# Eleven instead of seven pairs of the down projection with seven multiplications, their weight differences and token sums made in an earlier stage

## The chip, the core and the metric

The kernel runs on one core of a Trainium2 chip. The metric is the time of one execution on the device in microseconds (us); lower is better. Of the core's engines, TensorE (PE) multiplies 128x128 blocks, VectorE (DVE) and ScalarE (ACT) work on elements, GpSimd (POOL) and SyncE (SP) issue transfers (DMAs); "PEld" in the profile is PE's loading of the stationary operand.

## What is computed

One decoder block on 256 tokens and 16 meta tokens of width 2048: a recurrent branch and an attention branch, merged by gates and projected by `w_o`, and then a feed-forward part of width 5632. The change touches the last line of the reference, and uses what the line before it makes:

```python
h = h + merged @ w_o
gate, up = jnp.split(_rms(h, n2) @ w_gu, 2, axis=-1)
return h + (jax.nn.silu(gate) * up) @ w_dn        # w_dn: 5632 x 2048, float32
```

## The kernel before

**Split operands.** All matmuls run on float32r operands that are split in two: a high part (ACT copies float32 to float32r, `wh`) and a low part (DVE subtracts the high part from the float32 value, `wl`). A product of two such operands is three matmuls: high x high, low x high, high x low. Weights come from memory in raw tiles of 128x1024 float32 (512 KB; tag `raw`, four buffers), loaded by SP, and are split into `wh` and `wl` (four buffers each). `wload` (line 314) does this for a plain job, `split` for others.

**Jobs.** `run` takes a list of pairs (load, mul). It calls the load of a job and then the mul of the job before it. PE works in the order of the program. The orders of DVE, ACT, SP and POOL are made by the scheduler of the tile framework, so that loads and splits of later jobs stand well ahead of PE. Side work is written as generators: `spawn` starts one with a delay, each `yield` gives the time until its next step, and `slot`, called at each product, advances a clock made of the matmuls' own lengths and runs a step that has come due. This clock only decides where in the program the step is written.

**Gate and up** (lines 1385 to 1402). For each of eleven blocks `j` of 512 columns, `cm_jobs` multiplies the normed tokens `hts` with 512 columns of gate and then of up: 16 jobs of 8 pairs of matmuls (128x512 and 128x256), one raw tile a job. `post_gate` and `post_up` take the sums out of PSUM, multiply by the norm and by silu of the gate and split the product into `ach` and `acl`, the operand of the down projection: 44 blocks of 128 rows, 256 tokens.

**Down projection** (lines 1410 to 1572). Its 44 row blocks are taken in 22 pairs; the 2048 result columns in two halves `cg` of 1024. A pair and a half is a product of 2x2 blocks: two halves of 128 tokens and two row blocks, times two row blocks (`b11 b12`, `b21 b22`) and two groups of 512 columns. A plain pair (`slow_jobs`) makes eight products, 24 matmuls of 128x512, in two jobs with one raw tile each. A fast pair (`fast_jobs`) makes seven, 21 matmuls, from sums and differences of the blocks, in four jobs: `mul0` one product, `mul1`, `mul2` and `mul3` two each. Four of the products go to four PSUM banks of their own (`ps`, tile names `dnp`), the others to the four banks of the plain sums (`cs`, tile names `dn`); at the end of a half `sums_of_products` adds the four into the result `hh` (a copy by ACT and eight additions by DVE), and `post` adds the plain sums and stores.

Before the change pairs 0 to 6 are fast. Their weights lie in two raw tiles (1 MB a pair and half), and DVE makes four differences of 512 columns into `tt` (line 1515) between the splits. The sums and differences of tokens are made by `sums_of_pairs` (lines 1417 to 1446) on DVE from the split operand, in four batches beside the first jobs of the down projection; they are split into `sst`, which takes the memory of `hts`. `ORDER` puts eight plain pairs first and then fast and plain pairs in turn in the first half, and two plain pairs for each fast one in the second.

Of the kernel before, what the change touches and what calls it, by code (L numbers as in the profile page):

```python
# [18 lines left out]
P = 128  # L19
D = 2048  # L20
NMETA = 16
# [20 lines left out]
for _n, _k in (("n1", 16), ("mu", 24), ("mu_w", 1), ("mu_a", 1), ("mu_g", 2), ("w0", 8), ("a0", 8), ("k_k", 8),  # L42
# [19 lines left out]

LANES = 108
# [4 lines left out]
FAST = [0, 1, 2, 3, 4, 5, 6]  # L68
BATCHES = (2, 2, 2, 1)
SLOW = list(range(7, 22))  # L70
ORDER = [SLOW[:8] + [i for pair in zip(FAST, SLOW[8:]) for i in pair],
         [i for n, f in enumerate(FAST) for i in (SLOW[2 * n], f, SLOW[2 * n + 1])] + SLOW[14:]]
# [44 lines left out]
def hybrid_block(ctx, tc, A, out, dbg=None):  # L117
# [195 lines left out]

    def wload(parts, n, between=None, lay=None):
# [6 lines left out]
        if lay is not None:  # L321
# [14 lines left out]
            nc.vector.tensor_tensor(tl, rr, th.bitcast(F32), op=ALU.subtract)  # L336
# [967 lines left out]
    hts = hp.tile([P, KT, 2, L], F32R, tag="hts", name="hts")  # L1304
# [32 lines left out]
    for j in range(4):  # L1337
# [3 lines left out]
        def post(t, ps, j=j, js=js):  # L1341
            nc.vector.tensor_tensor(hh[:, t, js], ps, hh[:, t, js], op=ALU.add)
            jk = hp.tile([P, 512], F32, tag="jk", name=f"jk{j}{t}", bufs=2)
# [3 lines left out]
            for k in range(4 * j, 4 * j + 4):  # L1347
                pt = aux_ps(f"hT{k}")[:, :T]
                for t in range(2):
                    nc.tensor.transpose(pt[:, t * P:(t + 1) * P], hh[:, t, k * P:(k + 1) * P], ident)  # L1350
                tmp = hp.tile([P, T], F32, tag="htmp", name=f"htmp{k}", bufs=3)
                nc.vector.tensor_scalar(tmp, pt, vc("n2", k), None, op0=ALU.mult)
                split(hts[:, k, 0, NMETA:], hts[:, k, 1, NMETA:], tmp)
# [6 lines left out]
    obs = [hp.tile([P, P], F32, tag="ob", name=f"ob{t}", bufs=2) for t in range(2)]  # L1360
# [19 lines left out]
    acp = ap_pool.__enter__()  # L1380
    NF = DFF // P
    ach = acp.tile([P, NF, T], F32R, tag="ach", name="ach")
    acl = acp.tile([P, NF, T], F32R, tag="acl", name="acl")
    wgu = A["w_gate_up"][0]
    for j in range(DFF // 512):
# [8 lines left out]
        def post_up(pss, gs=gs, j=j):  # L1394
            for m, (g, ps) in enumerate(zip(gs, pss)):
# [5 lines left out]
        run(cm_jobs(wgu[:, j * 512:(j + 1) * 512], KT, hts, NMETA, T, post_gate, name=f"gt{j}"))  # L1401
        run(cm_jobs(wgu[:, DFF + j * 512:DFF + (j + 1) * 512], KT, hts, NMETA, T, post_up, alloc=aux_ps, name=f"up{j}"))
# [7 lines left out]
    wdn = A["w_down"][0]  # L1410
# [3 lines left out]
    sst = hp.tile([P, KT, 2, L], F32R, tag="hts", name="sst").rearrange("p k a t -> p (k a t)")  # L1414
    sst = sst[:, :len(fast) * 6 * P].rearrange("p (i s a c) -> p i s a c", i=len(fast), s=3, a=2)

    def sums_of_pairs():

        at = 0
        for n in BATCHES:  # L1420
            fs, ps_ = slice(at, at + n), slice(fast[at], fast[at] + n)
            at += n
            h = lambda k, t: acp_h[:, ps_, k, t, :].bitcast(F32)
            l = lambda k, t: acp_l[:, ps_, k, t, :].bitcast(F32)
            f = [sst[:, fs, i, 1, :] for i in range(3)] + [acp_l[:, ps_, 0, 1, :]]
            hi = [sst[:, fs, i, 0, :] for i in range(3)] + [acp_h[:, ps_, 0, 1, :]]
            f32 = [hp.tile([P, T], F32, tag="ga", name=f"s{at}{i}", bufs=8)[:, :n * P].rearrange("p (i c) -> p i c", c=P)
                   for i in range(4)]

            def tt(i, x_, y_, op):  # L1430
                nc.vector.tensor_tensor(f32[i], x_, y_, op=op)
            tt(0, h(0, 1), h(1, 1), ALU.add)
            tt(0, f32[0], l(0, 1), ALU.add)
            tt(0, f32[0], l(1, 1), ALU.add)
            tt(1, f32[0], h(0, 0), ALU.subtract)
            tt(1, f32[1], l(0, 0), ALU.subtract)
            tt(2, h(0, 0), h(0, 1), ALU.subtract)
            tt(2, f32[2], l(0, 0), ALU.add)
            tt(2, f32[2], l(0, 1), ALU.subtract)
            tt(3, h(1, 0), f32[1], ALU.subtract)  # L1440
            tt(3, f32[3], l(1, 0), ALU.add)
            yield PAIRS
            for i in range(4):
                nc.scalar.activation(hi[i], f32[i], AF.Copy)
                nc.vector.tensor_tensor(f[i], f32[i], hi[i].bitcast(F32), op=ALU.subtract)
            yield PAIRS
# [41 lines left out]
    def fast_jobs(i, cg, cs, ps, end):  # L1488
        box = {}

        def b(k, x_):
            return wdn[i * 256 + k * P:i * 256 + (k + 1) * P, cg * 1024 + x_ * 512:cg * 1024 + (x_ + 1) * 512]

        def load0():
            ra, rb = (wp.tile([P, 1024], F32, tag="raw", name="raw", bufs=RAWB) for _ in range(2))
            nc.sync.dma_start(ra, wdn[i * 256:i * 256 + P, cg * 1024:(cg + 1) * 1024])
            for x_ in range(2):
                nc.sync.dma_start(rb[:, (1 - x_) * 512:(2 - x_) * 512], b(1, x_))
            box["r"] = rows(ra), rows(rb)
            w = split_tiles()  # L1500
            split(*(t[:, 0:2] for t in w), box["r"][0][:, 0:2])
            return w

        def load1():
            w = split_tiles()
            split(*w, box["r"][1])
            return w

        def load2():
            (b11, b12), (b22, b21) = ([r[:, 0:2], r[:, 2:4]] for r in box["r"])  # L1510
            w, v = split_tiles(), split_tiles()
            ts = [rows(hp.tile([P, 1024], F32, tag="tt", name="tt", bufs=2)) for _ in range(2)]
            t1, t2, t3, t4 = (t[:, 2 * n:2 * n + 2] for t in ts for n in range(2))
# [122 lines left out]
```

## Time and profile before

| | |
|---|---|
| time, median of 3 runs | 1520.99 us (1520.26 to 1521.58) |
| profiled execution, span on the core | 1517.7 us (the page gives no other time for it) |
| granted PE clock | 1.00 throughout |
| gate and up | 788 to 1278 us, PE busy 490.0 of 490.0 |
| down projection | 1278 to 1514 us, PE busy 235.1 of 236.0 |
| bytes moved | 283.32 MB, mean 187 GB/s |
| landing of a 512 KB weight load | 4.3 us (gate and up), 5.3 us (down), medians |

The span runs from the first to the last instruction on the core; the time of a run holds a little more. A line of the groups reads: line of the kernel, engine, operation, result<-operands, shape, count, then busy time in us and the mean of one in ns, then the idle time of the engine just ahead of such instructions and who ended it. A line of the waits reads: engine, what waits, its line <- for whom, then us in all, times, and the longest.

### The profile page before, as it was taken

How to read it: one execution, taken by the hardware profiler on the slowest of the kernel's cores; microseconds unless marked ns; L12 is line 12 of the kernel's file. 1: busy time of each engine (PE TensorE's matmuls, PEld its weight loads, DVE VectorE, ACT ScalarE, POOL GpSimd, SP SyncE). 2: the span in 40 equal slices, each digit the busy share in tenths (PEclk: the TensorE clock that was granted, in tenths of full speed). 3: DMA queues.
4: the chain of work that ended last, by engine and by line, in shares of the span. 5: the costliest groups of instructions: out<-in, count | busy, mean ns of one | idle time of the engine just before them, and what ended most of it. 6: DMA issues, size and time to landing. Idle time of an engine off the chain costs nothing.

```text
span 1517.7 us, 26174 instructions
## 1 busy us (share of the span) xinstructions
PE 1509.9 (99%) x10071; PEld 1339.5 (88%) x10071; DVE 1112.0 (73%) x2009; ACT 808.3 (53%) x1230; POOL 99.3 (7%) x182
## 2 busy tenths in 40 slices
PE   9999999999999999999999999999999999999998
PEld 9999999999989888998888888888888888887887
DVE  7888699689789857875665666566566658879776
ACT  7664565475465545644554555454455545554543
POOL 2112202202202000000000000000000000000000
PEclk9999999999999999999999999999999999999999
DMA  8557456646645757777566666666666666566664
GB/s 271 166 166 212 119 156 185 170 122 173 188 127 149 223 152 214 234 231 240 181 179 192 189 187 193 191 186 192 190 187 191 193 186 182 178 211 201 213 206 138
DMA packets 210365, 283.32 MB, mean 187 GB/s; under 512 B 24320, under 2 KB 129296, under 8 KB 210240
## 3 DMA queue, kind: packets, MB, share of 16 engines
q1 hardware_dynamic: 205344, 277.25, 61.9%
q10 hardware_dynamic: 4896, 4.40, 0.9%
q8 instruction: 79, 1.29, 0.3%
q14 instruction: 46, 0.38, 0.1%
HBM read 274.36 MB, written 7.24 MB: 186 GB/s over the span
## 4 chain that ended last, share of the span: by engine, by line
PE 95%; DVE 3%; DMA 1%; issue 1%; ACT 0%; SPq 0%; DVEq 0%; ACTq 0%
PE up L441 11%; PE gt L441 11%; PE zg L441 8%; PE gt L443 5%; PE up L443 5%; PE dn L1461 4%; PE dn L1460 4%; PE dn L1462 4%; PE zg L443 4%; PE f L441 2%; PE br L365 2%; PE br L366 2%; PE br L367 2%; PE f L365 2%; PE wo L1329 2%; PE wo L1331 2%
## 5 line engine op out<-in xcount | busy, mean ns | idle before, releaser
L336 DVE TENSOR_TENSOR wl<-raw,wh 128x1024 fp32r<-128x1024 f32 x460 | 561.9, 1226 | 281.3 <-ACT wh L335 280.6
L335 ACT ACTIVATE wh<-raw 128x1024 fp32r<-128x1024 f32 x460 | 486.5, 1059 | 470.2 <-PE up L441 118.9
L441 PE MATMUL gt<-hts,wh 128*128 128x512 f32 x704 | 242.9, 393 | 0.0
L441 PE MATMUL up<-hts,wh 128*128 128x512 f32 x704 | 242.7, 392 | 0.0
L443 PE MATMUL gt<-hts,wl 128*128 128x256 f32 x660 | 184.8, 280 | 0.0
L443 PE MATMUL up<-hts,wl 128*128 128x256 f32 x660 | 184.6, 280 | 0.0
L441 PE MATMUL zg<-xhl,wh 128*128 128x512 f32 x512 | 181.2, 399 | 0.0
L441 PEld LDWEIGHTS up<-hts,wh 128*128 128x128 f32 x704 | 130.0, 188 | 25.2
L441 PEld LDWEIGHTS gt<-hts,wh 128*128 128x128 f32 x704 | 129.9, 188 | 25.1
L443 PE MATMUL zg<-xhl,wl 128*128 128x256 f32 x480 | 134.3, 280 | 0.0
L443 PEld LDWEIGHTS up<-hts,wl 128*128 128x128 f32 x660 | 125.3, 190 | 1.8
L443 PEld LDWEIGHTS gt<-hts,wl 128*128 128x128 f32 x660 | 125.3, 190 | 1.8
L441 PEld LDWEIGHTS zg<-xhl,wh 128*128 128x128 f32 x512 | 94.3, 188 | 18.7 <-issue 0.7
L1460 PE MATMUL dn<-wh,ach 128*128 128x512 f32 x282 | 110.7, 393 | 0.0
L1461 PE MATMUL dn<-wh,acl 128*128 128x512 f32 x282 | 110.6, 392 | 0.0
L1462 PE MATMUL dn<-wl,ach 128*128 128x512 f32 x282 | 110.5, 393 | 0.0
L443 PEld LDWEIGHTS zg<-xhl,wl 128*128 128x128 f32 x480 | 90.9, 189 | 1.2
L365 PE MATMUL f<-xhl,wh 128*128 128x272 f32 x256 | 75.9, 296 | 0.0
L367 PE MATMUL f<-xhl,wl 128*128 128x272 f32 x256 | 73.6, 288 | 0.0
L366 PE MATMUL f<-xhl,wh 128*128 128x272 f32 x256 | 73.6, 288 | 0.0
L1462 PEld LDWEIGHTS dn<-wl,ach 128*128 128x128 f32 x282 | 52.9, 187 | 12.3 <-DVE wl L336 0.3
L1461 PEld LDWEIGHTS dn<-wh,acl 128*128 128x128 f32 x282 | 52.9, 188 | 12.0
(493 smaller groups left out, 3056.7 us busy)
## 6 DMA issues: line engine op xcount, KB each, us to landing
raw<-in_w_gate_up_dram SPq DMA_DIRECT2D x176, 512.0 KB, 4.3
raw<-in_w_in_dram SPq DMA_DIRECT2D x160, 512.0 KB, 3.9
raw<-in_w_down_dram SPq DMA_DIRECT2D x74, 512.0 KB, 5.0
raw<-in_w_o_dram SPq DMA_DIRECT2D x32, 512.0 KB, 4.3
raw<-in_w_branch_a_dram SPq DMA_DIRECT2D x16, 512.0 KB, 4.6
raw<-in_w_branch_b_dram SPq DMA_DIRECT2D x16, 512.0 KB, 5.0
raw<-in_w_down_dram SPq DMA_DIRECT2D x28, 256.0 KB, 4.6
zgd<-zg ACTq DMA_DIRECT2D x30, 128.0 KB, 3.8
```

The lines of the kernel that those rows point to most:

```text
L335: nc.scalar.activation(th, rr, AF.Copy)
L336: nc.vector.tensor_tensor(tl, rr, th.bitcast(F32), op=ALU.subtract)
L365: nc.tensor.matmul(ps, wh, ah, start=first, stop=False)
L366: nc.tensor.matmul(ps, wh, al, start=False, stop=False)
L367: nc.tensor.matmul(ps, wl, ah, start=False, stop=last)
L441: nc.tensor.matmul(ps.rearrange("p (a t) -> p a t", a=2), wh, act, start=first, stop=last)
L443: nc.tensor.matmul(ps[:, :T], wl, act[:, 0, :], start=False, stop=False)
L1329: nc.tensor.matmul(o, ah[:, kt, ts_], hi, start=first, stop=False)
L1331: nc.tensor.matmul(o, ah[:, kt, ts_], lo_, start=False, stop=last)
L1460: nc.tensor.matmul(o, a[0], hi, start=first, stop=False)
L1461: nc.tensor.matmul(o, a[1], hi, start=False, stop=False)
L1462: nc.tensor.matmul(o, a[0], lo_, start=False, stop=last)
```

## The change

- Fast pairs are 0 to 10, plain pairs 11 to 21 (`FAST`, `SLOW`). In each half a lead of plain pairs comes first (`LEAD`: two, then one). Then, after each half of a fast pair, the number of plain jobs that keeps the two kinds in step; two plain jobs come last.
- `sums_of_weights`, a generator that starts in the first block of up, makes the differences of weights for all 22 combinations of fast pair and half. POOL loads the four blocks (1 MB, in two DMAs with rows of 2 KB) into `r`; DVE makes three subtractions (1024, 512 and 512 columns) into `v`; POOL stores `v` (1 MB) to the memory of the chip (`ts`). `r` and `v` have one buffer each. Each subtraction is put behind the last weight split written by then (`tc.issue_after(behind[0].ins)`). The steps are written 11000, 2600, 2600 and 1600 ns of the program's clock apart.
- `sums_of_tokens`, called in `post_up` for each fast pair, makes the four sums and differences of tokens (128 columns each) on DVE from the float32 product, and POOL stores them (`ss`, 256 KB).
- In the down projection a fast pair has four raw tiles: `b11` (256 KB), `b22` and `b21` (512 KB), and two loads of differences from `ts` (512 KB each). There is no subtraction of weights there any more. `split_of_sums` loads the token sums by POOL into `sl` (two buffers, up to two pairs each) and splits them into `sst`.
- Memory pools: `hts` moves into a pool of its own, with the high and the low part in two separate stretches of 4112 elements; the first parts of the stage, `r`, `v` and later `sst` and `sl` use pools one after the other. The last job of up is finished ahead of the down projection's pool in the program.

```diff
-FAST = [0, 1, 2, 3, 4, 5, 6]
-BATCHES = (2, 2, 2, 1)
-SLOW = list(range(7, 22))
+FAST = list(range(11))
+BATCHES = (2, 2, 2, 2, 2, 1)
+SLOW = list(range(11, 22))
+LEAD = (2, 1)
+LANDED = 11000
+DIFFER = 2600
+STORED = 1600
...
-    hts = hp.tile([P, KT, 2, L], F32R, tag="hts", name="hts")
+    hts = ht.tile([P, HTS], F32R, tag="hts", name="hts")[:, :2 * HPART].rearrange("p (a e) -> p a e", a=2)
+    hts = hts[:, :, NMETA:].rearrange("p a (k t) -> p k a t", t=T)
...
+    def sums_of_weights():
+        for cg in range(2):
+            for i in FAST:
+                r = pre.tile([P, 2, 1024], F32, tag="r", name="r", bufs=1)
+                for x_ in range(2):
+                    nc.gpsimd.dma_start(r[:, :, x_ * 512:(x_ + 1) * 512],
+                                        kblock(wdn[i * 256:(i + 1) * 256, cg * 1024 + x_ * 512:cg * 1024 + (x_ + 1) * 512]))
+                yield LANDED
+                v = pre.tile([P, 2, 2, 512], F32, tag="v", name="v", bufs=1)
+                b21, b22 = r[:, 1, :512], r[:, 1, 512:]
+                with tc.issue_after(behind[0].ins):
+                    nc.vector.tensor_tensor(v[:, 0], r[:, :, 512:], r[:, 0].rearrange("p (x c) -> p x c", x=2),
+                                            op=ALU.subtract)
+                yield DIFFER
+                with tc.issue_after(behind[0].ins):
+                    nc.vector.tensor_tensor(v[:, 1, 0], b22, v[:, 0, 0], op=ALU.subtract)
+                yield DIFFER
+                with tc.issue_after(behind[0].ins):
+                    nc.vector.tensor_tensor(v[:, 1, 1], b21, v[:, 1, 0], op=ALU.subtract)
+                d = tsd[i, cg] = dp.tile([4, P, 512], F32, tag=f"ts{i}{cg}", name=f"ts{i}{cg}")
+                nc.gpsimd.dma_start(d.rearrange("n p c -> p n c"), v.rearrange("p n x c -> p (n x) c"))
+                yield STORED
...
+        def load1():
+            r = fresh()
             for x_ in range(2):
-                nc.sync.dma_start(rb[:, (1 - x_) * 512:(2 - x_) * 512], b(1, x_))
+                nc.sync.dma_start(r[:, (1 - x_) * 512:(2 - x_) * 512], b(1, x_))
...
+        def sums(n):
+            def load():
+                r = fresh()
+                nc.sync.dma_start(r.rearrange("p (x c) -> p x c", x=2),
+                                  tsd[i, cg][2 * n:2 * n + 2].rearrange("x p c -> p x c"))
+                w = split_tiles()
+                split(*w, rows(r))
+                return w
...
+        plain = [job for i in SLOW for job in slow_jobs(i, cg, cs, i == SLOW[-1])]
+        run(plain[:2 * LEAD[cg]])
+        del plain[:2 * LEAD[cg]]
+        many, done = len(plain) - 2, 0
+        for n, i in enumerate(FAST):
+            jobs = fast_jobs(i, cg, cs, ps, i == FAST[-1])
+            for half in range(2):
+                run(jobs[2 * half:2 * half + 2])
+                upto = (2 * n + half + 1) * many // (2 * len(FAST))
+                run(plain[done:upto])
+                done = upto
+        plain = plain[done:]
+        run(plain)
```

The scheduler's order shows where this work went. On DVE in gate and up, before the change, between the end of one up block and the next gate block (L336 is the weight split; L1399, L511, L448 and L1391 belong to the two post functions):

```order
L1399 TENSOR_TENSOR ub_13956<-ub_13956,ga_13510 128x256
L1399 TENSOR_TENSOR ub_13963<-ub_13963,ga_13511 128x256
L336 TENSOR_TENSOR wl<-raw,wh 128x1024
L511 TENSOR_TENSOR acl<-ub_13956,ach 128x256
L511 TENSOR_TENSOR acl<-ub_13963,ach 128x256
L336 TENSOR_TENSOR wl<-raw,wh 128x1024 x5
L448 TENSOR_TENSOR ga_13916<-ga_13916,gt_0_13976 128x256
```

There the splits stand alone or among the post functions. The same engine in a late up block after the change (L343 is the split; L1413, L1417 and L1420 are the three subtractions of a block of weights):

```order
L1417 TENSOR_TENSOR v<-r,v 128x512
L343 TENSOR_TENSOR wl<-raw,wh 128x1024
L1420 TENSOR_TENSOR v<-r,v 128x512
L343 TENSOR_TENSOR wl<-raw,wh 128x1024 x5
L1413 TENSOR_TENSOR v<-r 128x1024
L343 TENSOR_TENSOR wl<-raw,wh 128x1024
L455 TENSOR_TENSOR ub_13360<-ub_13360,up_0_13173 128x256
```

The three subtractions of a block have one split between them, and five splits lie between the last of one block and the first of the next; that holds all through the stage. On POOL, which has no instruction in these stages before, the order at the end of up is now (L1422 stores v, L1407 loads r, L1484 loads token sums):

```order
L1422 DMA ts_14214<-v 128x4x512
L1407 DMA r<-in_w_down_dram 128x2x512 x2
L1422 DMA ts_14419<-v 128x4x512
L1484 DMA sl_14678<-ss_10311 128x512
L1484 DMA sl_14678<-ss_10332 128x512
L1484 DMA sl_14724<-ss_10751 128x512
```

Each store of v stands directly ahead of the two loads of the next r, and the first token sums are loaded right behind the last store. On SP at the start of the down projection, before (L326 a plain tile, L1496 and L1498 the two tiles of a fast pair):

```order
L326 DMA raw<-in_w_gate_up_dram 128x2x512 x176
L326 DMA raw<-in_w_down_dram 128x2x512 x16
L1496 DMA raw<-in_w_down_dram 128x1024
L1498 DMA raw<-in_w_down_dram 128x512 x2
L326 DMA raw<-in_w_down_dram 128x2x512 x2
```

And after (L333 a plain tile, L1543, L1551 and L1559 the four tiles of a fast pair):

```order
L333 DMA raw<-in_w_gate_up_dram 128x2x512 x176
L333 DMA raw<-in_w_down_dram 128x2x512 x4
L1543 DMA raw<-in_w_down_dram 128x512
L1551 DMA raw<-in_w_down_dram 128x512 x2
L1559 DMA raw<-ts_10259 128x2x512 x2
L333 DMA raw<-in_w_down_dram 128x2x512
```

Sixteen plain tiles ahead of the first fast pair became four, and a fast pair's two tiles became four.

132 lines of the change are left out of this document (64 added, 68 removed).

## The prediction

> **What bounds the kernel now.** I read the page first, for the engine that ends last: its span, its busy times and its chain by engine.
>
> ```profile
> span 1517.7 us, 26174 instructions
> PE 1509.9 (99%) x10071; PEld 1339.5 (88%) x10071; DVE 1112.0 (73%) x2009; ACT 808.3 (53%) x1230; POOL 99.3 (7%) x182
> PE 95%; DVE 3%; DMA 1%; issue 1%; ACT 0%; SPq 0%; DVEq 0%; ACTq 0%
> ```
>
> TensorE (PE) carries 95% of the chain, so fewer matmuls are worth what a matmul takes, as long as PE is fed. The change works in two stages, and the table of windows has one row for each: gate and up from 788 to 1278 us, the down projection after it.
>
> ```profile
> core 0: us, PE busy (x) PEld busy (x) DVE busy (x) ACT busy (x) POOL busy (x), PEclk, DMA share, GB/s
> 788.00:1278.00 490.00, 490.00 (x2830) 432.10 (x2829) 307.37 (x464) 246.88 (x356) 0.00 (x0) 1.00 0.66 189
> 1278.00:1514.00 236.00, 235.12 (x1018) 189.96 (x1016) 191.19 (x252) 118.90 (x136) 0.00 (x0) 1.00 0.60 190
> ```
>
> In gate and up PE has no gap at all, DVE is busy 307 of 490 us, POOL does nothing, and the transfers run at 189 GB/s. There is nothing to win there, only to lose. The list of waits of that window tells how far ahead the weight splits are:
>
> ```profile
> DVE wl L336 <- ACT wh L335: 183.6, 141, 1.8
> ACT wh L335 <- PE up L441: 117.9, 74, 1.7
> ```
>
> ACT waits for PE to give a weight tile back, DVE waits for ACT, and nobody waits for a transfer: splits run as far ahead as four tiles allow. The groups of that window give their size:
>
> ```profile
> L336 DVE TENSOR_TENSOR wl<-raw,wh 128x1024 fp32r<-128x1024 f32 x177 | 216.7, 1224 | 183.6 <-ACT wh L335 183.6
> L335 ACT ACTIVATE wh<-raw 128x1024 fp32r<-128x1024 f32 x176 | 186.8, 1062 | 229.2 <-PE up L441 117.9 <-PE gt L441 105.2 <-PE up L443 2.0
> ```
>
> One weight job (512 KB) comes every 490/177 = 2.77 us.
>
> **Matmuls saved.** A pair with seven multiplications has 21 matmuls of 128x512 per column half where a plain one has 24. Four more such pairs and two halves make 4 x 2 x 3 = 24 fewer; 1014 become 990. These two rows of the timeline are the first and the 119th matmul of an unbroken stretch of the down projection; the two below, of the instructions on its sums, hold the stage's first and last start.
>
> ```profile
> 1317.67 0.39 PE L1460 MATMUL dn<-wh,ach 128*128 128x512 f32 x1
> 1344.85 0.40 PE L1461 MATMUL dn<-wh,acl 128*128 128x512 f32 x1
> ```
> ```profile
> L1460 PE MATMUL dn<-wh,ach x282: 387/392/399, 1278.3 to 1513.0; 128*128 128x512 f32 x141
> L1462 PE MATMUL dn<-wl,ach x282: 391/392/501, 1278.8 to 1513.5; 128*128 128x512 f32 x141
> ```
>
> 27.18 us over 118 steps are 0.2303 us each (the 0.39 is a duration, overlapped with the next). The saving is 24 x 0.2303 = 5.5 us, all of it on PE's path.
>
> **The gap between the column halves.** 1513.5 - 1278.3 = 235.2 us, and 1013 steps of 0.2303 are 233.3: PE loses 1.9 us in this stage. The chain in order of time shows where:
>
> ```profile
> 1387.73 1.22 DVE wl L336
> 1389.55 0.60 DVE u L1553
> 1398.40 1.13 DVE wl L336
> 1401.27 1.82 DVE tt L1515 x3
> 1404.31 0.50 PE dnp L1460
> ```
>
> At the end of the first half DVE has twelve additions into hh, the splits, and the differences tt of the next fast pair; it is the engine that is late, and PE waits near 1404. After the change the twelve additions stay, the differences are gone from this stage. I take 1.2 of the 1.9 us as won; the ends are 0 and 1.9.
>
> **What gate and up get.** The groups that price the new DVE work are the old differences, 512 columns each, and the old token sums of one 128-column block:
>
> ```profile
> L1515 DVE TENSOR_TENSOR tt<-raw,tt 128x512 f32<-128x512 f32 x28 | 19.2, 686 | 11.5 <-DMA raw<-in_w_down_dram 11.4
> L1431 DVE TENSOR_TENSOR s<-s,acl 128x128 f32<-128x128 f32 x6 | 1.6, 288 | 0.1
> ```
>
> There are 22 blocks of weights (11 pairs, two column halves). Each has one subtraction of 1024 columns, as long as a split (1.22 us), and two of 512 (0.69): 22 x 2.6 = 57 us. Token sums are 11 x 4 x 0.288 = 13 us. DVE goes from 307 to 377 of 490 us, still under PE. What hides it: PE has three more jobs loaded when a split starts, 3 x 2.77 = 8.3 us less the 2.3 us of a split, so 6 us of cover. If a subtraction waits for its transfer longer than this, PE stands. I charge 0.5 us; the lower end is 0, since PE has no gap to lose there, the upper end is in the first rival. The differences are placed behind a split on DVE, so what queues behind a late one is the next split, and behind that PE.
>
> The moving operand of these matmuls has its two parts 4112 elements apart, where they were 272 apart. Both row shapes are 128x512 from one tile; I charge 0, with 1 us to either side. New memory pools add waits: the first write of sst waits for the last up matmul and for POOL's last block, but its first reader comes over 51 matmuls (12 us) into the stage, so 0. The lead before the first fast pair (four plain jobs, then two) and the last two plain jobs at the end are as long as what stood there, so the end stays.
>
> **What the down projection gets.** Its DVE work falls by the 56 differences (56 x 0.69 = 38 us) and most of the sums of pairs. Its loads grow: a fast pair reads 1.75 MB in four raw tiles, where it read 1 MB in two. The issue lists give the landing times, of gate and up first, then of the down projection:
>
> ```profile
> raw<-in_w_gate_up_dram SPq DMA_DIRECT2D x170, 512.0 KB, 4.3
> ```
> ```profile
> raw<-in_w_down_dram SPq DMA_DIRECT2D x68, 512.0 KB, 5.3
> raw<-in_w_down_dram SPq DMA_DIRECT2D x28, 256.0 KB, 4.6
> ```
> ```profile
> L511 DVE TENSOR_TENSOR wl<-raw,wh 128x512 fp32r<-128x512 f32 x14 | 9.6, 687 | 1.2 <-ACT wh L510 0.9
> L510 ACT ACTIVATE wh<-raw 128x512 fp32r<-128x512 f32 x14 | 8.9, 635 | 15.9 <-PE dn L1461 10.2 <-DMA raw<-in_w_down_dram 4.0 <-PE dnp L1461 1.7
> ```
>
> There are four raw tiles, and each is held from issue until its split has ended on DVE. After the lead the first half has 11 x 21 + 9 x 24 = 447 matmuls, 102.9 us, and 44 + 18 = 62 tiles: 1.66 us a tile, 6.64 us for a round of four. A 512 KB tile is held 4.3 + 1.06 + 1.22 = 6.6 us, a 256 KB one 4.6 + 0.64 + 0.69 = 5.9. So the ring of raw tiles just keeps pace if the landing is that of gate and up. With 5.3 us it is 7.6, the mean over 51 and 11 tiles is 7.3, and (7.3 - 6.64)/4 x 126 tiles (62 and 64) is about 20 us. But the 5.3 holds bursts: before, tiles were held through the differences and then issued two to four at a time. I take the lower landing and charge 1.6 us for late tiles and for the seven token-sum loads (256 KB each) that POOL still issues in this stage; ACT stands in front of the weight splits when one of these is late. The ends are 0 and 20.
>
> SP issues the same stores of the first half's result in front of the second half's loads; their wait was there before.
>
> **The sum.** -5.5 - 1.2 + 0.5 + 1.6 = -4.6 us. The page gives no time for the profiled execution but its span, 1517.7; the median of the runs, 1521.0, is 3.3 above it, and I keep that margin. 1517.7 - 4.6 + 3.3 = 1516.4.
>
> **First rival, the slower side: the weight blocks arrive late in gate and up.** Between the last subtraction of a block and the first of the next DVE has five splits, 5 x 2.77 - 0.69 = 13.2 us. In that time POOL must store 1 MB and load 1 MB into the one buffer, 2.10 MB, beside SP's weights. How fast two queues are together no stage of before shows; the nearest rows are the fastest stretch, the DMA view of 5 to 17 us, and the fastest 20 us of the down projection (PE alone listed, with clock, share and rate):
>
> ```profile
> DMA packets 1810, 4.68 MB, mean 390 GB/s; under 512 B 201, under 2 KB 201, under 8 KB 1809
> ```
> ```profile
> 1400.00:1420.00 20.00, 19.45 (x85) 1.00 0.76 251
> ```
>
> If POOL gets half, start and landing taken as 4.3 us less the 1.3 us that 0.52 MB takes at 390 GB/s: at 390 it needs 10.8 + 3.0 = 13.8 us, 0.6 late; at 251, 16.7 + 3.0 = 19.7, 6.5 late. The order gives a block 7 splits, sometimes 8, some 7.25 x 2.77 = 20.1 us; DVE is busy 0.627 x 20.1 + 2.6 + 0.6 = 15.8 of them, so 4.3 us can be made up. The point that decides is 290 GB/s in all. At 280 a block is 4.8 late, 0.5 more than can be made up, and 22 x 0.5 = 11 us are lost: 1516.4 + 11 = 1527.4. For it: one buffer each for r and v, and the share of gate and up, since 189 GB/s at 0.66 would make 286 at 1.00. Against it: the 390, and six microseconds of cover between DVE and PE.
>
> By the Trainium skill (DMA: Bandwidth & Descriptors, section Issuing engines are not separate DMA queues) POOL's and SP's transfers share the same 16 engines and interleave, which is this rival's mechanism; no run here shows it yet. SBUF — State Buffer (the Trainium skill), section Summary: rules for kernel authors, reckons about 358 GB/s for transfers between HBM and SBUF; the trace's 390 is above that. By 358 a block would be 11.7 + 3.0 = 14.7 us, 1.5 late, an estimate that stays within what DVE makes up, and the sum would be the same.
>
> **Second rival: the ring of raw tiles is the bound.** At a landing of 4.8 us a 512 KB tile is held 7.1, the mean is 6.9, and (6.88 - 6.64)/4 x 126 = 7.5 us are lost where I charge 1.6: -5.5 - 1.2 + 0.5 + 7.5 = +1.3, so 1522.3. For it: a half takes 66 tiles through the same four, where it took 44. Against it: evenly spaced loads queue less on each other.
>
> **Third: the scheduler undoes it,** moving differences in front of needed splits. The order shows them behind splits throughout; 4% is left for this and the rest, around no change.
>
> **How the numbers follow.** 0.2% is 3.0 us, about what a measurement of this kernel can tell from no change. The forecast has 47%, in a range of its own from 1513.6 (-5.5 - 1.9) to 1519: faster 0.40, same 0.07. The first rival has 29%: slower 0.26, same 0.03. The second has 20%: faster 0.02, same 0.11, slower 0.07. The rest: same 0.03, slower 0.01. Together 0.42, 0.24 and 0.34. The range runs from 1513.5 to 1531: below it lies almost nothing, above it the worse half of the first rival, somewhat over a tenth.
>
> **What would show it.** Right: 990 matmuls at 0.230 us; no PE gap between 788 and 1278; DVE near 377 us there, its subtractions waiting for the transfer of r by a microsecond or so; in the down projection landings of 512 KB under 4.5 us, and PE losing under 2 us. Wrong by the first rival: DVE's v waits for r by over 4 us in block after block, and PE shows gaps in gate and up. Wrong by the second: ACT waits for raw tiles all through the down projection, and PE for ACT.

## The result, and the profile after

The changed kernel takes 1553.89 us (median of 4 runs, 1552.46 to 1558.78) where the kernel before takes 1520.88 (4 runs, 1520.26 to 1521.58): a ratio of 1.0222, interval 1.0209 to 1.0234. It is slower by 33 us. The page of the changed kernel gives the span, the busy times and the chain by engine:

```profile
span 1550.8 us, 26501 instructions
PE 1524.3 (98%) x10047; PEld 1335.5 (86%) x10047; DVE 1142.8 (74%) x2035; ACT 820.1 (53%) x1242; POOL 160.4 (10%) x270
PE 74%; DMA 11%; issue 6%; DVE 5%; ACT 2%; POOL 1%; SPq 0%; ACTq 0%; DVEq 0%; POOLq 0%
```

PE has 24 matmuls fewer (10,047 against 10,071), as intended, and yet more busy time. The chain that ended last ran over PE for 95% before and does so for 74% now; transfers hold 11% of it. The table of windows, one row for each stage:

```profile
788.00:1292.50 504.50, 499.87 (x2828) 434.48 (x2827) 359.36 (x560) 243.45 (x355) 56.93 (x81) 1.00 0.84 282
1292.50:1546.50 254.00, 239.50 (x992) 183.60 (x990) 169.06 (x181) 134.69 (x149) 3.74 (x7) 0.99 0.76 252
```

Both stages are longer. The rows of the tiles hts and dn give their first and last matmuls. First hts before the change, then hts and dn after it:

```profile
L441 PE MATMUL gt<-hts,wh x704: 388/393/475, 788.8 to 1255.9; 128*128 128x512 f32 x176
L441 PE MATMUL up<-hts,wh x704: 388/393/398, 812.1 to 1278.1; 128*128 128x512 f32 x176
```
```profile
L448 PE MATMUL gt<-hts,wh x704: 387/395/629, 788.2 to 1269.8; 128*128 128x512 f32 x176
L448 PE MATMUL up<-hts,wh x704: 387/395/401, 811.7 to 1292.4; 128*128 128x512 f32 x176
```
```profile
L1506 PE MATMUL dn<-wh,ach x242: 387/394/794, 1292.6 to 1545.8; 128*128 128x512 f32 x121
L1508 PE MATMUL dn<-wl,ach x242: 387/393/794, 1293.1 to 1546.2; 128*128 128x512 f32 x121
```

Gate and up run from 788.2 to 1292.4, 504.2 us where it was 489.3 (788.8 to 1278.1): 14.9 more. The down projection's matmuls run from 1292.6 to 1546.2, 253.6 us where it was 235.2: 18.4 more, although 24 x 0.2303 = 5.5 us of work had gone. Its 990 steps of 0.2303 are 228.0 us, so PE loses 25.6 us there (counted in the same way, 1014 x 0.2303, it lost 1.6 us before; the windows row shows only 254.0 - 239.5 = 14.5 us as idle, since a matmul counts as busy for 0.39 us where the next could start after 0.23). The waits of the down projection, and below them its issue list, tell who is late:

```profile
ACT wh L517 <- DMA raw<-in_w_down_dram: 37.6, 22, 3.1
ACT wh L342 <- DMA raw<-in_w_down_dram: 29.4, 26, 2.8
ACT wh L517 <- DMA raw<-ts: 14.8, 34, 1.5
PEld dn L1508 <- DVE wl L343: 11.7, 14, 1.0
```
```profile
raw<-ts SPq DMA_DIRECT2D x44, 512.0 KB, 5.8
raw<-in_w_down_dram SPq DMA_DIRECT2D x40, 512.0 KB, 5.3
raw<-in_w_down_dram SPq DMA_DIRECT2D x63, 256.0 KB, 4.0
```

ACT waits 82 us, 82 times, for a raw tile, and PE in turn for the split: the sign that the prediction gave for its second rival. In gate and up, the waits and the landings:

```profile
ACT wh L342 <- DMA raw<-in_w_gate_up_dram: 111.6, 50, 6.4
DVE v L1413 <- DMA r<-in_w_down_dram: 8.5, 7, 3.0
PEld gt L450 <- DVE wl L343: 4.5, 3, 2.6
```
```profile
raw<-in_w_gate_up_dram SPq DMA_DIRECT2D x155, 512.0 KB, 6.8
r<-in_w_down_dram POOLq DMA_DIRECT2D x40, 512.0 KB, 9.9
```

The loads of the weights themselves land in 6.8 us (4.3 before) and ACT waits for them, where it never did. But the windows row above leaves only 504.5 - 499.87 = 4.6 us in which PE stood; the rest of the 14.9 us lies in a PE that is busy and slow. That shows best in a stretch without any gap. These are the rows of the window 1100 to 1200 us, of the kernel before and then of the changed one; the number in brackets behind PE's busy time counts its matmuls:

```profile
1100.00:1200.00 100.00, 100.00 (x578) 88.19 (x577) 64.86 (x101) 50.76 (x74) 0.00 (x0) 1.00 0.66 189
```
```profile
1100.00:1200.00 100.00, 100.00 (x569) 87.00 (x568) 67.46 (x97) 46.66 (x67) 10.98 (x15) 1.00 0.84 286
```

PE is at 100.00 and at a clock of 1.00 in both, with 1.6% fewer matmuls. By their starts, 16 pairs of matmuls (two weight tiles) take 5.550 us before and 5.647 after; I call 16 pairs a job from here on, and gate and up have 88 of them: 8.5 us. The pace differs from the start: the first two jobs take 6.449 and 5.547 us before and 6.477 and 5.579 after, and POOL starts its first load behind them, at 803.4.

So there were three suspects: the pace of gate and up (8 us; of the operands of these matmuls the change lays out hts anew, while the tiles `wh` and `wl` keep their addresses), PE's gaps there (4.6 us and what lies around them; POOL's transfers), and the down projection (25.6 us lost; the ring of raw tiles).

### The profile page after: what moved, and what is told of

Same layout as the page of the kernel before. It is cut to its first block, busy times and chain, and to the rows that moved or that the text cites. A ratio compares the mean times of both kernels' runs of the same rounds, so it can differ in the third digit from the quotient of the medians.

```text
span 1550.8 us, 26501 instructions
## 1 busy us (share of the span) xinstructions
PE 1524.3 (98%) x10047; PEld 1335.5 (86%) x10047; DVE 1142.8 (74%) x2035; ACT 820.1 (53%) x1242; POOL 160.4 (10%) x270
## 4 chain that ended last, share of the span: by engine, by line
PE 74%; DMA 11%; issue 6%; DVE 5%; ACT 2%; POOL 1%; SPq 0%; ACTq 0%; DVEq 0%; POOLq 0%
PE zg L448 8%; PE up L448 7%; PE gt L448 7%; DMA raw<-ts 4%; PE zg L450 4%; PE up L450 4%; DMA raw<-in_w_down_dram 4%; PE gt L450 3%; DMA raw<-in_w_gate_up_dram 2%; PE f L448 2%; PE br L372 2%; PE br L373 2%; PE br L374 2%; PE f L372 2%; PE wo L1341 2%
## 5 line engine op out<-in xcount | busy, mean ns | idle before, releaser
L343 DVE TENSOR_TENSOR wl<-raw,wh 128x1024 fp32r<-128x1024 f32 x444 | 543.2, 1227 | 246.2 <-ACT wh L342 234.5
L342 ACT ACTIVATE wh<-raw 128x1024 fp32r<-128x1024 f32 x444 | 468.9, 1059 | 481.3 <-DMA raw<-in_w_gate_up_dram 111.6
L448 PE MATMUL gt<-hts,wh 128*128 128x512 f32 x704 | 248.2, 397 | 0.0
L448 PE MATMUL up<-hts,wh 128*128 128x512 f32 x704 | 246.4, 395 | 0.0
L448 PE MATMUL zg<-xhl,wh 128*128 128x512 f32 x512 | 181.2, 400 | 0.0
L448 PEld LDWEIGHTS gt<-hts,wh 128*128 128x128 f32 x704 | 130.7, 189 | 28.0
L448 PEld LDWEIGHTS up<-hts,wh 128*128 128x128 f32 x704 | 130.0, 188 | 27.8
L518 DVE TENSOR_TENSOR wl<-raw,wh 128x512 fp32r<-128x512 f32 (+1 forms) x88 | 95.3, 1091 | 53.0 <-ACT wh L517 48.1
L517 ACT ACTIVATE wh<-raw 128x512 fp32r<-128x512 f32 (+1 forms) x88 | 83.4, 952 | 68.9 <-DMA raw<-in_w_down_dram 37.6
L448 PEld LDWEIGHTS zg<-xhl,wh 128*128 128x128 f32 x512 | 94.3, 188 | 18.5 <-issue 0.7
L1508 PE MATMUL dn<-wl,ach 128*128 128x512 f32 x242 | 97.7, 404 | 7.1 <-DVE wl L343 5.8
L1506 PE MATMUL dn<-wh,ach 128*128 128x512 f32 x242 | 97.0, 401 | 5.8 <-ACT wh L342 3.0
L1507 PE MATMUL dn<-wh,acl 128*128 128x512 f32 x242 | 95.5, 394 | 0.0
```

What stands on the lines that cost most here:

```text
L342: nc.scalar.activation(th, rr, AF.Copy)
L343: behind[0] = nc.vector.tensor_tensor(tl, rr, th.bitcast(F32), op=ALU.subtract)
L448: nc.tensor.matmul(ps.rearrange("p (a t) -> p a t", a=2), wh, act, start=first, stop=last)
L517: nc.scalar.activation(hi, src, AF.Copy)
L518: nc.vector.tensor_tensor(lo_, src, hi.bitcast(F32), op=ALU.subtract)
L1506: nc.tensor.matmul(o, a[0], hi, start=first, stop=False)
```

## The experiments

### The distance of the two parts of hts alone, in the kernel before

```diff
-    hts = hp.tile([P, KT, 2, L], F32R, tag="hts", name="hts")
+    hts = hp.tile([P, KT, 2, L], F32R, tag="hts", name="hts").rearrange("p k a t -> p (k a t)")
+    hts = hts[:, :2 * (KT * T + NMETA)].rearrange("p (a e) -> p a e", a=2)
+    hts = hts[:, :, NMETA:].rearrange("p a (k t) -> p k a t", t=T)
...
-                split(hts[:, k, 0, NMETA:], hts[:, k, 1, NMETA:], tmp)
+                split(hts[:, k, 0], hts[:, k, 1], tmp)
...
```

> The kernel before with one edit: hts keeps its tile, but its high and low parts stand 4112 elements apart instead of 272, as in the changed kernel. Theory (the distance of the two parts sets the pace of gate and up): the pair of matmuls in gate and up goes from 0.347 to 0.353 us, 1408 pairs x 0.006 = 8.4 us more in gate and up, about 1529 us. Rival (the pace comes from where the new pools put the tiles, or from the new work beside gate and up): 0.347 us per pair as before, 1521 us within 1 us.

Measured: 1522.88 us, ratio 1.0014 (1.0004 to 1.0023). Its rows of hts:

```profile
L441 PE MATMUL gt<-hts,wh x704: 388/394/480, 789.1 to 1258.4; 128*128 128x512 f32 x176
L441 PE MATMUL up<-hts,wh x704: 390/394/399, 812.5 to 1280.7; 128*128 128x512 f32 x176
```

Gate and up take 491.6 us, 2.3 more than before, at 5.576 us per job. The distance costs something, but a quarter of what was to be explained: the theory as I had it fell.

### The parts 256 apart, in the changed kernel

```diff
-    hts = ht.tile([P, HTS], F32R, tag="hts", name="hts")[:, :2 * HPART].rearrange("p (a e) -> p a e", a=2)
-    hts = hts[:, :, NMETA:].rearrange("p a (k t) -> p k a t", t=T)
+    hts = ht.tile([P, KT, 2, T], F32R, tag="hts", name="hts")
```

> The changed kernel with one edit: hts has its two parts 256 elements apart, side by side for each k. Theory (distance): the pair of matmuls in gate and up goes back to about 0.347 us, 8.4 us less, about 1545.5 us; the gaps at 870 to 990 us (6.5 us) and the stalls in down (about 24 us) stay. Rival (pools or neighbours set the pace): 0.353 us per pair as in the changed kernel, about 1554 us.

Measured: 1552.45 us, ratio 1.0208 (1.0193 to 1.0223), not told apart from the changed kernel. The job took 5.585 to 5.60 us, faster by 0.05, but its windows row shows that PE then stood 8 us where it stood 4.6:

```profile
788.00:1293.30 505.30, 497.24 (x2828) 432.46 (x2827) 358.78 (x559) 242.05 (x355) 56.94 (x81) 1.00 0.84 282
```

What PE saved in pace it gave back waiting. In gate and up the pace and the late transfers are two limits that cover each other, not two terms of a sum.

### No weight differences made in gate and up

```diff
-            spawn(sums_of_weights(), HOP)
...
-                                  tsd[i, cg][2 * n:2 * n + 2].rearrange("x p c -> p x c"))
+                                  kblock(wdn[i * 256:(i + 1) * 256, cg * 1024 + n * 512:cg * 1024 + (n + 1) * 512]))
```

> The changed kernel without the weight differences in gate and up: no loads of r, no DVE differences, no stores. Down reads rows of w_down in their place, as many bytes and transfers, and so computes another product. Theory: the gaps of PE in gate and up (6.5 us) go, since the raw loads land in about 4.3 us again instead of 6.8; the pace of 0.353 us per pair stays (layout), and down keeps its 24 us of stalls (ring of raw tiles): about 1547 us. Rival A (the stream also slows the pace): gate and up fall by 14.9 us, about 1539 us. Rival B (down stalls because its sums lie in the DRAM tiles that were stored late, or because POOL's queue is still busy): down falls too, by 10 us or more.

Measured: 1550.49 us, ratio 1.0196 (1.0181 to 1.0211). The windows rows of its two stages, and the landing in gate and up:

```profile
788.00:1285.40 497.40, 497.40 (x2826) 432.75 (x2826) 311.15 (x492) 246.86 (x355) 8.35 (x15) 1.00 0.66 194
1285.40:1542.40 257.00, 241.39 (x993) 182.90 (x991) 168.97 (x181) 134.59 (x149) 3.80 (x7) 0.99 0.75 248
```
```profile
raw<-in_w_gate_up_dram SPq DMA_DIRECT2D x155, 512.0 KB, 4.2
```

PE has no gap left in gate and up, the landing is 4.2 us again, and the stage is 6.6 us shorter (787.8 to 1285.4, 497.6 us). The remaining 8.3 us are pace, so the stream of blocks doesn't cause that; and the down projection is no faster, so it isn't slowed by where the differences lie or by POOL's blocks. The token sums were still made and stored in this run.

### No loads of the weight differences in down

```diff
-                r = fresh()
-                nc.sync.dma_start(r.rearrange("p (x c) -> p x c", x=2),
-                                  tsd[i, cg][2 * n:2 * n + 2].rearrange("x p c -> p x c"))
-                split(*w, rows(r))
+                split(*w, rows(hh[:, 0, :1024]))
```

> The changed kernel with the weight differences made and stored, but not loaded in down: the splits of these 44 tiles read a resident tile instead, so down computes another product. All matmuls, splits and instruction orders stay; 44 of 147 raw loads (22 of 51 MB) go. Theory (the ring of four raw tiles and the landing of 5.3 to 5.8 us bound down): PE's stalls in down fall from about 24 us to under 3 us, landing falls under 5 us, about 1531 us. Rival (the splits and their order on ACT and DVE bound down: each product waits for a split that is queued behind others): stalls stay at 15 us or more, 1545 us or more.

Measured: 1529.95 us, ratio 1.0061 (1.0046 to 1.0076), 24 us less than the changed kernel. The down projection's windows row and its longest wait:

```profile
1293.60:1526.40 232.80, 230.79 (x993) 186.73 (x991) 167.47 (x181) 133.08 (x149) 3.74 (x7) 0.99 0.54 177
```
```profile
ACT wh L517 <- PE dn L1507: 63.6, 43, 2.9
```

It takes 232.5 us, a loss of 4.5 us instead of 25.6, and ACT waits for PE instead of for transfers. The splits and their order, all still there, are not the bound. What is left is the ring of raw tiles or the bytes themselves, since this run took both away; the run with a ring of its own, below, parts them.

### The address of hts: three kernels

In the kernel before, hts starts at byte 75,648 of a partition, 384 behind a multiple of 512; in the changed one the new pools put it at 87,040, a multiple of 512. The first of these kernels is the kernel before with the parts far apart and the changed kernel's remainder, the second the changed kernel with the old remainder, the third the kernel before with its own distance and the new remainder.

```diff
+    shift = hp.tile([P, 288], F32, tag="shift", name="shift")
+    nc.vector.memset(shift, 0.0)
...
```

The dummy tile `shift` has 288, 96 and 160 elements in the three.

> The kernel before with the parts of hts 4112 elements apart, as in the first experiment, and the tile 1152 bytes further on in SBUF, so that its start has the same remainder by 2 KB as in the changed kernel. Theory (the address of hts, with the distance of its parts, sets the pace): a job of 16 pairs in gate and up goes from 5.576 us (distance alone) to about 5.65 us, 88 jobs x 0.07 = 6 us more than the first experiment, about 1529 us. Rival (the pace follows what else the changed kernel moved, or settles in one of several rhythms by chance): 5.58 us per job, about 1523 us.

> The changed kernel with hts 384 bytes further on in SBUF (same remainder by 512 bytes as in the kernel before). Theory (address): a job of 16 pairs in gate and up falls from about 5.65 to about 5.58 us, some 6 us less, about 1548 us. Rival: 5.60 to 5.65 us as in the changed kernel, about 1554 us.

> The kernel before with its own layout of hts (parts 272 elements apart), the tile 640 bytes further on in SBUF, so that its start is a multiple of 512 bytes as in the changed kernel (75,648 has a remainder of 384). Theory (address and distance act together, through the address by 512 bytes): the job of 16 pairs leaves 5.550 us; by the size that the address alone made with the parts far apart (5.576 to 5.650), up to 5.63 us, 88 x 0.075 = 6.6 us more, 1523 to 1527 us. Rival (the address matters only with the parts 4112 apart): 5.550 us as before, 1521 us.

Measured: 1528.72 us, ratio 1.0053 (1.0038 to 1.0068); 1551.06 us, 1.0205 (1.0188 to 1.0221); 1521.44 us, 1.0007 (0.9998 to 1.0015). The window 1100 to 1200 of the three, in this order, PE at 100.00 in each:

```profile
1100.00:1200.00 100.00, 100.00 (x569) 86.97 (x568) 61.33 (x92) 50.26 (x74) 0.00 (x0) 1.00 0.64 185
```
```profile
1100.00:1200.00 100.00, 100.00 (x575) 87.61 (x575) 65.73 (x94) 44.34 (x66) 10.81 (x15) 1.00 0.83 284
```
```profile
1100.00:1200.00 100.00, 100.00 (x577) 88.06 (x576) 64.68 (x101) 50.74 (x74) 0.00 (x0) 1.00 0.64 188
```

The jobs by the starts of their first matmuls (the mean of the four steps that repeat; the far parts and the old one have 64 bytes ahead of the data, those 256 apart none):

| elements apart | start, remainder by 512 | us per job of 16 pairs | in |
|---|---|---|---|
| 272 | 384 | 5.550 | before, the last three below |
| 272 | 0 | 5.560 | third of these |
| 4112 | 384 | 5.576 | first experiment, second of these |
| 4112 | 0 | 5.647 | first of these, changed kernel |
| 256 | 0 | 5.585 to 5.60 | second experiment |
| 256 | 384 | 5.643 | nine pairs, 256 apart, below |

The kernel before, given the distance and the remainder of the changed one, runs at the changed one's pace to the nanosecond: its jobs take 5.654, 5.653, 5.653 and 5.626 us in turn in both. With the remainder put back the changed kernel runs at the pace of the first experiment. So distance and address together make the 8.3 us, 2.3 by the distance and 6.0 by the address on top of it. With the old distance the address costs 0.9 us (88 x 0.010), as the rival of the third expectation had it. In the second kernel only some 2 us of the gain reached the end of the stage (502.1 us for 504.2): PE's standing grew to 502.4 - 496.5 = 5.9 us by its windows row, as it did in the run with 256.

```profile
788.00:1290.40 502.40, 496.49 (x2828) 432.05 (x2827) 359.02 (x560) 242.33 (x355) 57.09 (x81) 1.00 0.84 284
```

With the far parts at a multiple of 512 there is a second rhythm: a job can go on at 5.59 us, with nothing else changed. The changed kernel fell into it near 845 us, with PE at 100% in that stretch, and came back to 5.65 behind a gap. Why the layouts differ isn't visible in the trace, and I found no simple rule that covers all six lines of the table. Nor is 512 shown to be the right unit: the second line's tile stands 512 bytes behind a multiple of 1024, the fourth line's on one, and no run parts the two.

### A ring of their own for the stored differences

```diff
+        def fresh(own=False):
+            if own:
+                return dn.tile([P, 1024], F32, tag="rs", name="rs", bufs=3)
...
-BATCHES = (2, 2, 2, 2, 2, 1)
+BATCHES = (1,) * 11
...
```

> The changed kernel, but down loads the stored weight differences into a ring of three tiles of their own beside the four raw tiles (the token sums are loaded by single pairs into one small tile to make room). All work and all bytes stay. Theory (the ring of four raw tiles, refilled only as splits free it, bounds down): PE's stalls in down fall from about 24 us to under 5 us, about 1534 us. Rival (the 58 MB themselves, on one queue at 251 GB/s, bound it, so that deeper buffers only lengthen the landing): stalls stay at 15 us or more, landing of the differences rises over 7 us, 1545 us or more.

Measured: 1537.45 us, ratio 1.0116 (1.0099 to 1.0133), 16 us less than the changed kernel. The windows row of its down projection, the landing of the differences, and a wait that had been small:

```profile
1292.00:1528.60 236.60, 231.74 (x993) 184.79 (x991) 168.95 (x191) 133.46 (x159) 5.42 (x10) 1.00 0.82 275
```
```profile
rs<-ts SPq DMA_DIRECT2D x44, 512.0 KB, 5.2
```
```profile
ACT sst L517 <- DMA sl<-ss: 22.2, 10, 3.7
```

From 1292.2 to 1528.6 are 236.4 us: a loss of 8.4 instead of 25.6, with the same bytes, moved at 275 instead of 252 GB/s and landing no later. So the ring was the bound and neither the queue nor the rate: 17 us. PE stands in one place only, 1310 to 1350 us, at the first fast pairs, where ACT waits in order for the token sums; they come pair by pair in this run, to make room.

### Nine pairs, the blocks spread wider

```diff
-FAST = list(range(11))
-LANDED = 11000
+FAST = list(range(9))
+LANDED = 15000
...
```

> As the last one, with nine fast pairs instead of eleven (1002 matmuls in down instead of 990, 2.8 us more), a ring of four for the differences, and the step behind a block's loads 15 us long instead of 11, so that 18 blocks are spread over gate and up instead of 22. Theory (POOL's transfers beside the raw loads make the gaps in gate and up): the gaps fall from 6.5 to under 3 us; with down's stalls gone about 1532 us. Rival (gaps come from the DVE differences tied behind splits, however far apart the blocks): gaps stay at 5 us or more, about 1536 us.

Measured: 1532.87 us, ratio 1.0076 (1.0057 to 1.0094). Of the window 870 to 990, the changed kernel's row and then this one's:

```profile
870.00:990.00 120.00, 115.61 (x645) 100.00 (x644) 83.65 (x139) 52.64 (x79) 15.99 (x23) 0.99 0.82 275
```
```profile
870.00:990.00 120.00, 119.75 (x679) 103.86 (x679) 87.30 (x145) 57.32 (x82) 14.42 (x21) 1.00 0.80 270
```

PE stood 4.4 us there and stands 0.25 now. That fits the theory, but with fewer pairs the token sums are fewer too; the last runs below come back to it. Down lost 7.1 us (1284.4 to 1522.3, 237.9 against 1002 x 0.2303 = 230.8), again at its first fast pairs. The profiled run is the fastest of the four, 1528.32, so the median holds some us that these rows don't show.

### Everything so far together, twice

```diff
-LEAD = (2, 1)
+LEAD = (4, 1)
...
+    shift = ht.tile([P, 96], F32, tag="shift", name="shift")
...
```

> The changed kernel with what the runs pointed to: hts 384 bytes further on, nine fast pairs with 18 blocks spread by a step of 15 us, three tiles of their own for the stored differences, four plain pairs ahead of the first fast one. Sum by the runs: gate and up 88 x 5.577 = 490.8 us and 2 us of gaps, against 489.3 us of the kernel before; down 1002 x 0.2303 = 230.8 us and 2 to 4 us of stalls, against 235.2 us: 0 to 4 us more than before, 1521 to 1525 us. Rival (the gaps in gate and up grow again as PE runs faster, as in the run with the shift alone): 1526 to 1530 us.

> As the last one, but with the parts of hts 256 elements apart and the tile 896 bytes further on (same remainder by 512 bytes as in the kernel before). Theory (address and distance): a pace between 5.550 and 5.59 us per job, since 256 apart at a multiple of 512 bytes gave 5.585 to 5.595; 1519 to 1525 us. Rival (256 apart has a rhythm of its own at any address): 5.59 us, about 1 us more than the last one.

Measured: 1524.7 us, ratio 1.0031 (1.002 to 1.0042), and 1531.82 us, ratio 1.0076 (1.0062 to 1.0089). The second expectation was wrong: 256 apart at the old remainder gave the slow 5.643 us, so the remainder that is good for one distance is bad for another. In the first one gate and up kept the forecast (493.0 us, with 0.8 us of standing), and down lost 6.0 us, where 2 to 4 had been expected. The chain of the changed kernel in order of time shows what such a loss is made of:

```profile
1315.42 5.62 DMA sl<-ss
...
1321.07 0.03 ACT sst L517
...
1321.79 0.95 ACT wh L517
1322.74 0.04 issue
1322.79 0.79 PE dn L1506
```

This load of token sums takes 5.6 us; ACT stands for the last 2.9 of them, the weight split that PE needs stands behind it on ACT, and PE behind that. Over the whole stage ACT waited 4.1 us for such loads in the changed kernel, and 22.2 in the run above where they came pair by pair.

### Token sums made in down, as before, with nine, ten and eleven pairs

```diff
-    hts = ht.tile([P, HTS], F32R, tag="hts", name="hts")[:, :2 * HPART].rearrange("p (a e) -> p a e", a=2)
...
+    hts = ht.tile([P, KT, 2, L], F32R, tag="hts", name="hts")
...
-    spawn(split_of_sums(), GAP)
+    spawn(sums_of_pairs(), 2 * PAIRS)
```

> Nine fast pairs as in the last two runs, with the token sums made in down from ach and acl as in the kernel before (no loads of sl, no token sums in gate and up); the memory that this frees holds hts in the layout of before (272 apart, same remainder by 512 bytes) and a fourth tile for the stored differences. Theory (the last 5 to 6 us of stalls in down are ACT standing in order behind the loads of the token sums): stalls in down 1 to 2 us, gate and up 88 x 5.55 = 488.4 us and 1.5 us of gaps; 1517.5 to 1520.5 us. Rival (what is lost there is the splits and sums themselves, ahead of the first fast pairs): stalls of 4 us or more stay, 1522 us or more.

> The same with ten fast pairs (996 matmuls in down, 1.4 us less than with nine) and 20 blocks with a step of 13 us. Theory (gaps of gate and up grow with the rate of POOL's blocks): gaps of 2 to 3 us, so no better than nine: 1517 to 1521 us. Rival (with the token sums gone from POOL and DVE the blocks fit): gaps under 1.5 us, 1516 to 1518 us.

> The same with eleven fast pairs as in the changed kernel (990 matmuls in down), 22 blocks with its step of 11 us, three tiles for the stored differences. Theory (rate of the blocks): gaps of 6 to 8 us in gate and up, down at 228.0 us and 1 to 3 us of stalls; 1521 to 1525 us. Rival (the gaps came with the token sums as well): gaps under 3 us, 1516 to 1519 us.

Measured: 1515.55 us, ratio 0.9969 (0.9958 to 0.9981); 1514.5 us, 0.9961 (0.9948 to 0.9973); 1516.09 us, 0.9972 (0.996 to 0.9984). All three are faster than the kernel before, by 0.3 to 0.4%. The windows rows of the one with ten pairs, then of the one with eleven:

```profile
788.00:1277.60 489.60, 489.60 (x2828) 431.68 (x2827) 353.49 (x523) 244.95 (x356) 44.25 (x60) 1.00 0.84 275
1277.60:1507.60 230.00, 230.00 (x999) 186.82 (x997) 175.83 (x221) 130.19 (x152) 0.00 (x0) 1.00 0.79 264
```
```profile
788.00:1280.20 492.20, 491.36 (x2828) 431.65 (x2827) 354.65 (x529) 242.36 (x356) 48.65 (x66) 1.00 0.84 282
1280.20:1508.90 228.70, 228.70 (x993) 185.73 (x991) 182.07 (x239) 134.03 (x160) 0.00 (x0) 1.00 0.82 272
```

PE has no gap in down in any of them, so the last 4 to 8 us there were the loads of the token sums, in front of which ACT stood; with the sums made by DVE in that very stage (171 to 182 us busy of 229 to 231) no such gap is left. In gate and up ten pairs leave no gap either, against my theory, and eleven leave 0.8 us, and 2.6 us in all over ten: the rival held, the gaps had come with the token sums as well. The changed kernel's own trace has this too. Its token sums are made from 836 to 1073 us, and PE stands 4.6 us between 870 and 1073; from 1073 on the blocks go on at the same rate and PE doesn't stand:

```profile
990.00:1073.00 83.00, 82.75 (x471) 71.86 (x470) 63.57 (x102) 41.48 (x60) 10.65 (x16) 1.00 0.94 325
1073.00:1180.00 107.00, 107.00 (x608) 93.09 (x607) 75.53 (x109) 51.46 (x75) 11.38 (x16) 1.00 0.85 287
1180.00:1290.00 110.00, 110.00 (x625) 95.70 (x624) 76.65 (x110) 53.88 (x79) 11.72 (x17) 1.00 0.85 285
```

Without the blocks, in the third experiment, the token sums alone left no gap; without the token sums the eleven pairs' blocks alone left 0.8 us. Most of it takes both. The token sums are 11 stores by POOL and 13 us on DVE (44 of 0.286); which of the two mattered wasn't tried. Against the kernel before, ten pairs save 18 x 0.2303 = 4.1 us of matmuls and 1.2 us of the old gap, 5.3 in all; the spans differ by 1517.7 - 1512.3 = 5.4. Ten and eleven pairs are not told apart firmly (1514.4 to 1515.2 against 1514.4 to 1517.8).

## Why the prediction was wrong, point by point

The span went from 1517.7 to 1550.8, 33.1 us, where -4.6 had been forecast. By the runs this is +8.3 for the pace of hts, +6.6 for the stream of blocks on top of it, and in down -5.5 for the matmuls and 25.6 - 1.6 = +24.0 for what PE lost there: 33.4, and gate and up began 0.6 us earlier. The first two cover each other in part, so their split holds only in this order.

- **The 24 matmuls: right.** 990 remain, and with eleven pairs and no waits down takes 228.4 us (1280.5 to 1508.9) where 990 x 0.2303 = 228.0 is the least.
- **The gap between the halves, 1.2 of 1.9 us won: right, where nothing else is late.** Counted alike, the loss was 235.2 - 1014 x 0.2303 = 1.6 us before and is 0.4 with eleven pairs and no late loads. In the changed kernel it couldn't be seen under the new waits.
- **The distance of the parts of hts, charged 0 with 1 us to either side: wrong, 8.3 us.** "Both row shapes are 128x512 from one tile" was a reason about the shape, and it said nothing about where the tile lies. The distance itself cost 2.3 us. The new pools also move hts by 11,392 bytes, and I didn't price that at all; on top of the distance it was the larger part, 6.0 us.
- **Gate and up, charged 0.5 us: wrong, 6.6 us.** I asked whether the blocks would come late for DVE. They mostly didn't: v waited for r 8.5 us in all, in 7 places, never over 3.0. What came late were the weights on SP's own queue, 6.8 us instead of 4.3, and ACT waited 111.6 us for them. The first rival had the place and the sharing of the transfers right, and the wrong victim; and the token sums, which I had priced at DVE's 13 us alone, were part of it. By the Trainium skill (DMA: Bandwidth & Descriptors, section Issuing engines are not separate DMA queues) transfers run on the same 16 DMA engines and interleave, whichever engine started them. The landings agree: 6.8 us beside POOL's blocks, and 4.2 us once the blocks were taken away.
- **Down, charged 1.6 us: wrong by most, and the step is named in the prediction.** I took the lower landing, since "evenly spaced loads queue less on each other". They landed in 5.3 and 5.8 us. Put into the prediction's own formula, with 8.1 us held for 44 tiles of differences (5.8 + 1.06 + 1.22), 7.6 for 38 plain ones, 5.3 for 22 of 256 KB (4.0 + 0.64 + 0.69) and 6.3 for 22 loaded in two parts (4.0 + 1.06 + 1.22), the mean is 7.14 and (7.14 - 6.64)/4 x 126 = 16 us, near the 17 that the own ring took away (25.6 - 8.4). The second rival's mechanism was right. The 20 us that the prediction gave as the upper end of this term was about the size; the 7.5 us of the rival was not.
- **The token-sum loads,** lumped into the 1.6 us, were 4 to 8 us by themselves: that is what down still lost in the kernels that had the token sums loaded and the ring relieved, less the 0.4 us that stay without them. "ACT stands in front of the weight splits when one of these is late" was the right mechanism, with no price of its own.
- **The margin of 3.3 us between span and median came out, 1553.9 - 1550.8 = 3.1, by luck.** The 1550.8 belong to the run of 1552.46 us, the fastest of the four, so its own margin is 1.7; the other 1.4 us are the spread of the runs.

Down alone, 18.4 us longer where 5.1 less had been forecast, puts the sum at 1516.4 + 23.5 = 1540. So the range was too narrow even for its own terms: it ended at 1531, though the end of 20 us for the late tiles would have made 1535. On top of that each rival was priced with the other terms at rest; both came true at once, and a term charged at nothing with them.

## What to carry to other kernels

When a ring of buffers "just keeps pace" at the best landing time, price it at the landing the trace shows in that very stage: in-flight tiles over held time is the rate, and more tiles cured it here, where the queue still had room. Of an operand that only moves or is laid out anew, put the old remainder of its address and the old distances back before anything else is blamed, and look for a stretch in which PE is at 100% and count its matmuls. A load whose reader sits on an in-order engine in front of the bound engine's feed was dearer here than remaking the data on an engine that had the time.

## What the runs showed of the hardware that was not expected

- The pace of float32 matmuls without any wait depends on where the moving operand lies: 5.550 to 5.647 us for the same 32 matmuls at the same granted clock, a spread of 1.7%, over the six layouts tried: three distances of its two parts (256, 272, 4112 elements) at two remainders of its start by 512 bytes. One layout repeated its pace to the nanosecond in different kernels.
- For one layout there can be two steady rhythms (5.647 and 5.59 us per job), and a kernel can change from one to the other, mostly behind a gap of PE.
- A longer landing need not make PE stand longer: with eleven pairs and the token sums in down, the weights of gate and up landed in 7.3 us (median) and PE stood 0.8 us, where in the changed kernel 6.8 us went with 4.6.

```profile
raw<-in_w_gate_up_dram SPq DMA_DIRECT2D x155, 512.0 KB, 7.3
```
